# Row-maximum products of the next head, issued singly over the key steps

## The chip, the cores and the metric

The kernel runs on one core of a Trainium2 chip. The metric is the device time of one execution in microseconds; the median over several executions is compared. TensorE does the matmuls, VectorE (DVE) and GpSimd (POOL) elementwise work and reductions, ScalarE (ACT) the exponentials and copies, and SP issues most of the DMAs. Each engine works through its own list of instructions in order.

## The reference

Two layers over 2048 latent and 256 context tokens of width 1024. A layer normalises and modulates its input, projects it to 2816 columns, and runs four mixers: Fourier, attention, a short convolution and pooling. Each is gated by a SiLU; the gated outputs are concatenated and go through one output projection, and a residual is added. The part that matters here is the attention: four query heads of 64 channels on two key heads, for latent tokens

```python
sc = jnp.einsum('bqkgd,bskd->bkgqs', qi, k_all, preferred_element_type=jnp.float32)
p = jax.nn.softmax(sc, axis=-1).astype(v_all.dtype)
return jnp.einsum('bkgqs,bskd->bqkgd', p, v_all)
```

over all 2304 keys; context tokens attend to the 256 context keys alone, and only in the first layer.

## The kernel before

Tokens are in five blocks: block 0 has the 256 context tokens, blocks 1 to 4 have 512 latent tokens each. One head of one block is an object `Head` (called a head below): the first layer has 20 (blocks 1, 2, 3, 4, 0), the second 16. Numbers are split into a high and a low fp16 part, so a product takes two or three passes.

A head has two generators. `front` prepares it: one DMA loads its queries (qb), four transposes (L922) and a copy (L924) give qhh, then for each of four groups of 128 queries come five products with the keys (L931, one of 256 and four of 512 columns) and a reduction of each to row maxima (L932). Then comes the ending: the maxima are combined (L935), scaled into qb (L936), transposed (L939) and copied to qlm (L941). The maxima serve as the shift of the exponentials. `main` runs over the keys in 18 steps of 128 (2 steps for block 0). A step makes the scores in two matmuls (L972 with qhh, L973 with qlm, which brings the shift), two exponentials on ScalarE (L977, L978), a subtraction (L979, on GpSimd in even steps and on VectorE in odd ones) and the value products of the step before (L967) and of the one before that (L965). `back` and `close` normalise, gate and store a head's output while the next head runs.

PSUM has four tags with two banks each: st for scores, mx for the products of the maxima and for transposes, pv for value products, fl for what runs beside. `attention` runs the heads in turn and calls the next head's `front` from within `main`, at the steps of a tuple.

Beside the attention runs a fill: gates and local groups first (`local_groups`, L307), and later the output projection (`project`, L1125). It comes in groups of six matmuls of 512 columns. `spread` hands them out:

```python
past = [mark[0]] * (lag + 1)
for i in range(total):
    steps(gen, 1)
    past = past[1:] + [mark[0]]
    with tc.issue_after(past[0]), tc.issue_after(load_mark[0] or past[0]):
        steps(fill, n * (i + 1) // total - n * i // total)
```

`mark[0]` is the TensorE instruction that the source set last, a score's L972 or a product's L931, and `issue_after` keeps the fill's matmuls behind the mark of the step before (lag 1). The order on each engine is not that of the source: a scheduler takes instructions by their place in the source as soon as a model of the timeline finds them ready, within such edges.

The calls of a layer: `keys_values` loads keys in five steps and values in six; `opening` runs the first head's front under the value loads; then `spread(att, fill, ...)` runs all heads but those of the last two blocks beside the local groups. `project_setup` loads and splits w_out, 12 attention steps are run with no fill between, and then the remaining heads run beside the projection of the earlier blocks (96 groups over 71 steps in the first layer, 64 over 132 in the second). This place is called the takeover below.

Of the kernel before, what the change touches and what calls it, by code (L numbers as in the profile page):

```python
# [42 lines left out]
def hybrid_kernel(ctx: ExitStack, tc: tile.TileContext, T, out):  # L43
# [296 lines left out]
    def layer_blocks(L):  # L340
        return list(range(5)) if L == 0 else list(range(1, 5))
# [565 lines left out]
    class Head:  # L907
# [5 lines left out]
        def front(self):  # L913
            b, h, tp, kvs = self.b, self.h, self.tp, self.kvs
            g0, n = BLK[b]
            nt = n // 128
            kv = h // 2
            qb = tp.tile([128, 4, QW], F16, tag="qb", name="qb")[:, 0:nt]
            load_mark[0] = SP.dma_start(out=qb[:, :, 0:192], in_=qd[g0 // 128:(g0 + n) // 128, :, h].rearrange("t p c -> p t c")).ins
            pt = mx_bank(F16)  # L920
            for t in range(nt):
                PE.transpose(out=pt[:, t * 128:(t + 1) * 128], in_=qb[:, t, 0:128], identity=id16)  # L922
            qhh = tp.tile([128, 512], F16, tag="qhh", name="qhh")[:, 0:n]
            ACT.copy(out=qhh, in_=pt[:, 0:n])  # L924
            yield
            keys = [kvs["kc"][:, 0, kv, :]] + ([] if b == 0 else [kvs["kst"][kv][:, i * 512:(i + 1) * 512] for i in range(4)])
            mp = sm.tile([128, 4, 5], F32, tag="mp", name="mp")
            for t in range(nt):
                for i, kk in enumerate(keys):
                    ps = mx_bank()[:, 0:kk.shape[-1]]  # L930
                    mark[0] = PE.matmul(out=ps, lhsT=qhh[:, t * 128:(t + 1) * 128], rhs=kk, start=True, stop=True).ins  # L931
                    DVE.tensor_reduce(out=mp[:, t, i:i + 1], in_=ps, axis=AX.X, op=ALU.max)  # L932
                yield
            mr = sm.tile([128, 4], F32, tag="mr", name="mr")[:, 0:nt]
            DVE.tensor_reduce(out=mr, in_=mp[:, 0:nt, 0:len(keys)], axis=AX.X, op=ALU.max)  # L935
            DVE.tensor_scalar(out=qb[:, :, 192], in0=mr, scalar1=-1.0 / MROW, scalar2=PSHIFT * LOGIT / MROW, op0=ALU.mult, op1=ALU.add)  # L936
            pt = mx_bank(F16)
            for t in range(nt):
                PE.transpose(out=pt[0:65, t * 128:(t + 1) * 128], in_=qb[:, t, 128:193], identity=id16)  # L939
            qlm = tp.tile([128, 512], F16, tag="qlm", name="qlm")[:, 0:n]  # L940
            DVE.tensor_copy(out=qlm[0:65, :], in_=pt[0:65, 0:n])  # L941
            self.q = qhh, qlm
# [76 lines left out]
    def attention(heads):  # L1019

        o32 = [None]
        for _ in heads[0].front():
            yield
        for i, hd in enumerate(heads):
            ahead = heads[i + 1].front() if i + 1 < len(heads) else iter(())
            for j, _ in enumerate(hd.main()):
                if j == 1 and i:
                    heads[i - 1].back(o32)
                if j == (1 if heads[i].b == 0 else 3) and i:
                    heads[i - 1].close(o32)  # L1030
                if hd.b == 0 or j in (0, 2, 4, 7, 10, 13):
                    next(ahead, 0)
                yield
            yield from ahead
        heads[-1].back(o32)
        heads[-1].close(o32)

# [98 lines left out]
    def steps(gen, n):  # L1136
        for _ in range(n):
            if next(gen, 0) == 0:
                return

    def chain(*gens):
        for g in gens:
            yield from g
# [4 lines left out]
    with ExitStack() as st:  # L1148
        tp = TagPool(st, tc, "s0", {**TOKEN, "x": 4, "xn": 2, "h32": 2, "row": 1})
        ws = []  # L1150
        ahead = prep(0, 0, tp, aux_bank)
# [16 lines left out]
        for b in range(5):  # L1168
            ahead = prep(0, b + 1, tp, aux_bank) if b + 1 < 5 else iter(())
# [6 lines left out]
    def spread(gen, fill, total, n, lag=0):  # L1176
# [8 lines that stand above are left out]
    def weave(gen, n, other, m):  # L1185

        for i in range(n):
            steps(gen, 1)
            steps(other, m * (i + 1) // n - m * i // n)
            yield  # L1190
        yield from gen
        yield from other

    def opening(load, att):

        for i, _ in enumerate(load):
            if i < 5:
                steps(att, 1)
            yield 1

    for L in range(DEPTH):
        blocks = sorted(layer_blocks(L), key=lambda b: b == 0)
        nb = len(blocks)
        GATES = 148 * nb // 5
        zst = ExitStack()
        gates = gate_groups(L, TagPool(zst, tc, f"z{L}", {"z": 1}), gate_w[L])
        with ExitStack() as st:
            tags = {"acc0": 1, "acc1": 1, "part": 1} if L == 0 else {}
            tags.update({"u": 5, "wf": 1, "wm": 2, "t32": 3, "td": 3, "osb": 1, "dtab": 1, "tab": 1, "pq800": 1, "pq801": 1, "pq810": 1, "pq811": 1})
            if L:  # L1210
                tags.update({"dtab": 2, "tab": 2, "td": 4})
            fp = TagPool(st, tc, f"f{L}", tags)
            mods = chain(*(modulate(i, c, pv_bank, fp) for i, c in ([(0, 4), (0, 5)] + [(1, c) for c in range(6)] if L == 0 else [])))
            work = weave(fourier(L, fp), 24, mods, 32)
            steps(gates, 6)
            spread(work, gates, 24, GATES - 6, 4)
            steps(work, 1 << 30)
            if L == 0:
                affine(1)
        right = ExitStack()  # L1220
        ap = TagPool(right, tc, f"a{L}", {"zt": 2, "p32": 2, "qb": 2, "qhh": 2, "qlm": 2, "ph": 3, "pl": 3, "acc": 1, "o32": 1}, "right")
        kvs = {}
        att = attention([Head(L, kvs, b, h, ap) for b in blocks for h in range(4)])
        with ExitStack() as st:
            lp = TagPool(st, tc, f"l{L}", {"e": 8, "ht": 2, "hb": 2, "hu": 2, "pw32": 1, "pw": 2, "dh": 1, "dl": 1})
            fill = chain(gates, local_groups(L, lp))
            m = 8 * 4 * nb - GATES
            load = keys_values(L, ap, kvs)
            spread(load, fill, 5, 15, 0)
            spread(opening(load, att), fill, 6, 18, 1)  # L1230
            early = blocks[:-2]
            n, m = 72 * len(early), 8 * 4 * nb + 3 + m - 15 - 18
            spread(att, fill, 80, m * 80 // n, 1)
            with tc.issue_after(load_mark[0]):
                out_scale(L)
            spread(att, fill, n - 80, m - m * 80 // n, 1)
            steps(fill, 1 << 30)
        zst.close()
        with ExitStack() as st:
            tp = TagPool(st, tc, f"p{L}", {"mix": 1, "ml": 2, "ot": 1, "gate": 1, "x": 2})  # L1240
            project_setup(L, kvs)
            steps(att, 12)
            fill = project(L, early, tp)
            spread(att, fill, sum(72 if b else 11 for b in blocks[-2:]) - 12, sum(BLK[b][1] // 16 for b in early), 1)
            steps(fill, 1 << 30)
            steps(att, 1 << 30)
            right.close()
            late = project(L, blocks[-2:], tp)
            if L + 1 < DEPTH:
                with ExitStack() as st2:  # L1250
                    sp = TagPool(st2, tc, f"s{L + 1}", {**TOKEN, "s": 2, "x": 2, "xn": 1, "h32": 2}, "right")
                    with tc.issue_after(load_mark[0]):
                        block = token_groups(L + 1, sp, [])
                    for b in blocks[0:2]:
                        for _ in prep(L + 1, b, sp, mx_bank):
                            steps(late, 3)
                    for i, b in enumerate(blocks):
                        ahead = prep(L + 1, blocks[i + 2], sp, mx_bank) if i + 2 < 5 else iter(())
                        if i == 4:
                            gate_w[L + 1] = load_w(L + 1, *GATE_W[0:2], True)  # L1260
                        for _ in block(b):
                            steps(ahead, 1)
                            steps(late, 8)
                        steps(ahead, 9)
                        if i == 0:
                            steps(late, 1 << 30)
            steps(late, 1 << 30)
# [98 lines left out]
```

## Time and profile before

| what | us |
|---|---|
| median of 3 executions | 2276.16 |
| lowest and highest | 2273.22, 2279.15 |
| the profiled execution | 2273.57 |
| its span, first to last instruction | 2271.8 |
| TensorE, busy | 2158.7 |
| VectorE, busy | 1407.4 |
| ScalarE, busy | 1227.9 |
| GpSimd, busy | 936.1 |

The profile is of one execution. Busy time is the time in which an engine works on at least one instruction; a matmul of 512 columns shows some 380 ns, and the next one can start 0.22 us behind it, so the sum of durations says little. A wait is put down to the instruction that released the engine. The granted clock is the share of TensorE's full clock in a stretch.

### The profile page before, as it was taken

To read this page: it belongs to the slowest core of one execution; us is meant where nothing else is said; L and a number is where in the kernel's file an instruction comes from. 1 tells how busy PE (TensorE), PEld (TensorE's weight loads), DVE (VectorE), ACT (ScalarE), POOL (GpSimd) and SP (SyncE) were. 2 spreads that over 40 slices of the span, in tenths; PEclk is the share of its full clock that TensorE was granted. 3 is DMA by queue.
4 is the path that set the end of the run, shared out by engine and by line. 5 is a ranking of instruction groups with operands and counts; after the bars stand their busy time and mean duration, and the time that the engine had idled before them with its cause. 6 is when DMAs were issued, how large, how long until landed. Compare 5 with 4: busy or idle time off the path is not lost.

```text
span 2271.8 us, 41300 instructions
## 1 busy us (share of the span) xinstructions
PE 2158.7 (95%) x16327; PEld 1292.0 (57%) x16327; DVE 1407.4 (62%) x2639; ACT 1227.9 (54%) x2297; POOL 936.1 (41%) x996
## 2 busy tenths in 40 slices
PE   7999899989998999999999989999999999899999
PEld 3997556545555555545557984554454555455554
DVE  3655886366768767666465545413567776787743
ACT  4653454346777766544445624323467766566640
POOL 2786542215454455422125862011344556333320
PEclk9999999999999999999999999999999999999999
DMA  8424455510322110223474424323124210222133
GB/s 317 145 92 129 151 178 171 182 53 26 113 76 81 54 31 28 95 79 114 141 237 134 136 76 137 112 104 103 35 70 141 70 37 31 65 74 72 61 117 121
DMA packets 164081, 237.97 MB, mean 105 GB/s; under 512 B 28618, under 2 KB 113966, under 8 KB 163886
## 3 DMA queue, kind: packets, MB, share of 16 engines
q1 hardware_dynamic: 141294, 205.95, 27.2%
q10 hardware_dynamic: 22592, 29.37, 4.2%
q8 instruction: 128, 2.10, 0.4%
q14 instruction: 67, 0.55, 0.1%
HBM read 165.94 MB, written 69.34 MB: 104 GB/s over the span
## 4 chain that ended last, share of the span: by engine, by line
PE 68%; DVE 9%; ACT 4%; POOL 4%; issue 3%; DMA 2%; SPq 0%; POOLq 0%; DVEq 0%; ACTq 0%
PE fl L307 19%; PE fl L1125 15%; PE st L307 6%; PE pv L967 4%; PE st L972 4%; PE st L973 4%; PE mx L931 4%; DVE mp L932 2%; PE pv L965 2%; PE pv L329 1%; PE st L329 1%; PE mx L853 1%; DVE pl L979 1%; POOL pl L979 1%; PE mx L683 1%
## 5 line engine op out<-in xcount | busy, mean ns | idle before, releaser
L979 POOL TENSOR_TENSOR pl<-p,ph 128x512 f16<-128x512 f32 (+1 forms) x292 | 361.8, 1239 | 577.6 <-ACT p L978 515.1
L307 PE MATMUL fl<-h,w 128*128 128x512 f16 (+1 forms) x2592 | 582.1, 370 | 12.6 <-ACT w L147 9.3
L307 PEld LDWEIGHTS <-w 128*128 128x128 f16 x3456 | 331.5, 99 | 373.1 <-issue 22.2
L977 ACT ACTIVATE ph<-st 128x512 f16<-128x512 f32 (+1 forms) x584 | 350.9, 601 | 223.0 <-PE st L973 214.7
L932 DVE TENSOR_REDUCE mp<-mx 128x1 f32<-128x512 f32 (+1 forms) x648 | 388.8, 626 | 123.3 <-PE mx L931 112.7
L1125 PE MATMUL fl<-wo,ml 128*128 128x512 f16 x1632 | 376.8, 379 | 2.5 <-DVE ml L148 2.5
L978 ACT ACTIVATE p<-st 128x512 f32<-128x512 f32 (+1 forms) x584 | 351.2, 601 | 29.7 <-DVE pl L979 20.2
L979 DVE TENSOR_TENSOR pl<-p,ph 128x512 f16<-128x512 f32 (+1 forms) x292 | 231.9, 794 | 124.3 <-ACT p L978 100.0
L1125 PEld LDWEIGHTS <-ml 128*128 128x128 f16 x1632 | 157.4, 98 | 182.1 <-DVE ml L148 3.7
L967 PE MATMUL pv<-V,ph 128*128 128x130 f16 x2320 | 230.0, 221 | 6.9 <-ACT ph L977 6.2
L967 PEld LDWEIGHTS <-ph 128*128 128x128 f16 x2320 | 170.4, 98 | 116.4 <-ACT ph L977 29.1
L931 PE MATMUL mx<-kst,qhh 128*128 128x512 f16 x512 | 191.3, 385 | 22.9 <-DVE mp L932 22.1
L972 PE MATMUL st<-qhh,kst 128*128 128x512 f16 x512 | 195.6, 382 | 7.1 <-ACT p L978 6.2
L973 PE MATMUL st<-qlm,k 65*128 65x512 f16 x512 | 196.8, 384 | 0.0
L307 PE MATMUL st<-h,w 128*128 128x512 f16 (+1 forms) x864 | 189.1, 369 | 0.0
L965 PE MATMUL pv<-V,pl 128*128 128x66 f16 x2320 | 173.0, 194 | 12.5 <-DVE pl L979 6.0
L329 PEld LDWEIGHTS <-h 128*128 128x128 f16 x1632 | 160.0, 98 | 19.9 <-POOL h L269 1.1
L965 PEld LDWEIGHTS <-pl 128*128 128x128 f16 x2320 | 134.3, 98 | 65.0 <-POOL pl L979 14.0
L319 PEld LDWEIGHTS <-h 128*128 128x128 f16 x1728 | 99.5, 98 | 1.4 <-issue 0.6
L931 PEld LDWEIGHTS <-qhh 128*128 128x128 f16 x648 | 62.5, 99 | 65.8 <-issue 25.5
L329 PE MATMUL pv<-w,h 128*128 128x256 f16 x816 | 95.0, 275 | 0.9 <-POOL h L269 0.9
L329 PE MATMUL st<-w,h 128*128 128x256 f16 x816 | 92.7, 273 | 0.0
(303 smaller groups left out, 2903.7 us busy)
## 6 DMA issues: line engine op xcount, KB each, us to landing
wm<-in_w_mod_dram SPq DMA_DIRECT2D x48, 512.0 KB, 4.7
wst<-in_w_in_dram SPq DMA_DIRECT2D x44, 512.0 KB, 5.0
mix<-mixd SPq DMA_DIRECT2D x34, 512.0 KB, 4.0
zd<-z SPq DMA_DIRECT2D x64, 256.0 KB, 2.2
wst<-in_w_out_dram SPq DMA_DIRECT2D x32, 512.0 KB, 4.3
xt<-in_x_dram SPq DMA_DIRECT2D x20, 512.0 KB, 4.7
xd<-xt SPq DMA_DIRECT2D x18, 512.0 KB, 2.8
xt<-xd ACTq DMA_DIRECT2D x18, 512.0 KB, 3.7
```

What stands on the lines that cost most here:

```text
L307: PE.matmul(out=ps, lhsT=w[:, wp, k, :], rhs=h_ap(b, hp, k, 0, n), start=(k == 0 and i == 0), stop=(k == KC - 1 and i == 2))
L329: PE.matmul(out=ps[:, t], lhsT=h_ap(b, hp, k, (2 * i + t) * 128, 128), rhs=w[:, :, wp, k, :], start=(k == 0 and j == 0), stop=(k == KC - 1 ...
L931: mark[0] = PE.matmul(out=ps, lhsT=qhh[:, t * 128:(t + 1) * 128], rhs=kk, start=True, stop=True).ins
L932: DVE.tensor_reduce(out=mp[:, t, i:i + 1], in_=ps, axis=AX.X, op=ALU.max)
L965: PE.matmul(out=pv[t // 2][:, t % 2, 0:66], lhsT=p, rhs=v[:, 0:66], start=False, stop=(kt == nk - 1), skip_group_check=True)
L967: PE.matmul(out=pv[t // 2][:, t % 2, :], lhsT=p, rhs=v, start=(kt == 0 and t % 2 == 0), stop=False, skip_group_check=True)
L972: mark[0] = PE.matmul(out=ps, lhsT=self.k_tile(0, kt), rhs=qhh, start=True, stop=False).ins
L973: PE.matmul(out=ps, lhsT=self.k_tile(1, kt)[0:65, :], rhs=qlm[0:65, :], start=False, stop=True)
L977: ACT.activation(out=ph, in_=ps, func=ACTF.Exp, scale=1.0 / LOGIT)
L978: ACT.activation(out=p32, in_=ps, func=ACTF.Exp, scale=1.0 / LOGIT)
L979: (POOL if kt % 2 == 0 else DVE).tensor_tensor(out=pl, in0=p32, in1=ph, op=ALU.subtract)
L1125: PE.matmul(out=ps, lhsT=ml[:, mp, k, :], rhs=wo[k][:, wp, half * 512:(half + 1) * 512], start=(k == 0 and j == 0), stop=(k == KC - 1 and ...
```

## The change

`front` yields after each product and not after each group of five. `attention` takes 22 calls of the next front (4 if it is of block 0) and hands them out evenly over the key steps up to step 16 (up to step 1 in block 0). `opening` runs three calls of the first front under each of the six value loads, where it ran one under each of the first five. The number of steps of the first part of the attention grows by three, as three of the front's calls are left for it.

```diff
                     mark[0] = PE.matmul(out=ps, lhsT=qhh[:, t * 128:(t + 1) * 128], rhs=kk, start=True, stop=True).ins
                     DVE.tensor_reduce(out=mp[:, t, i:i + 1], in_=ps, axis=AX.X, op=ALU.max)
-                yield
+                    yield
...
-        for _ in heads[0].front():
-            yield
+        yield from heads[0].front()
         for i, hd in enumerate(heads):
             ahead = heads[i + 1].front() if i + 1 < len(heads) else iter(())
+            want = 2 + (2 if heads[i + 1].b == 0 else 20) if i + 1 < len(heads) else 0
+            last, done = 1 if hd.b == 0 else 17, 0
             for j, _ in enumerate(hd.main()):
...
-                if hd.b == 0 or j in (0, 2, 4, 7, 10, 13):
+                while done < want * (j + 1) // last:
                     next(ahead, 0)
+                    done += 1
                 yield
-            yield from ahead
+            for _ in ahead:
+                pass
...
-        for i, _ in enumerate(load):
-            if i < 5:
-                steps(att, 1)
+        for _ in load:
+            steps(att, 3)
             yield 1
...
-            n, m = 72 * len(early), 8 * 4 * nb + 3 + m - 15 - 18
+            n, m = 72 * len(early) + 3, 8 * 4 * nb + 3 + m - 15 - 18
```

## Rows read from the trace of the kernel before

**Rows 1.** The page's first part: busy us (share of the span) xinstructions.
```profile
PE 2158.7 (95%) x16327; PEld 1292.0 (57%) x16327; DVE 1407.4 (62%) x2639; ACT 1227.9 (54%) x2297; POOL 936.1 (41%) x996
```

**Rows 2.** Windows by stage: length, each engine's busy us, granted clock, DMA.
```profile
490.00:936.00 446.00, 426.46 (x3506) 245.00 (x3503) 316.17 (x518) 314.06 (x613) 228.73 (x244) 0.99 0.17 56
936.00:972.00 36.00, 30.32 (x186) 14.80 (x185) 26.06 (x47) 12.81 (x23) 6.11 (x6) 0.98 0.45 140
972.00:1160.00 188.00, 186.22 (x1265) 98.15 (x1264) 107.91 (x188) 86.71 (x163) 44.32 (x43) 0.98 0.38 125
1610.00:1940.00 330.00, 310.81 (x2477) 172.52 (x2474) 234.54 (x368) 230.09 (x445) 173.59 (x177) 1.00 0.20 67
1940.00:1968.00 28.00, 20.09 (x110) 8.61 (x109) 21.58 (x39) 8.88 (x17) 4.30 (x5) 0.87 0.33 106
1968.00:2190.00 222.00, 215.74 (x1815) 122.04 (x1815) 159.39 (x260) 144.70 (x277) 80.21 (x69) 0.99 0.19 62
```

**Rows 3.** Waits of TensorE, whole span: total us, times, longest us.
```profile
PE mx L931 <- DVE mp L932: 24.4, 57, 1.6
...
PE pv L965 <- DVE pl L979: 6.0, 9, 1.8
...
PE mx L939 <- DVE qb L936: 2.4, 2, 1.2
...
PE st L973 <- DVE qlm L941: 1.1, 4, 0.3
```

**Rows 4.** Waits of TensorE, first opening, 440 to 490 us.
```profile
PE mx L931 <- DVE mp L932: 2.9, 8, 1.2
```

**Rows 5.** Waits of TensorE, second opening, 1560 to 1610 us.
```profile
PE mx L931 <- DVE mp L932: 3.0, 10, 0.6
```

**Rows 6.** Waits of TensorE, first takeover, 936 to 972 us.
```profile
PE mx L931 <- DVE mp L932: 2.7, 5, 0.9
```

**Rows 7.** Waits of TensorE, second takeover, 1940 to 1968 us.
```profile
PE mx L931 <- DVE mp L932: 4.5, 8, 1.6
```

**Rows 8.** The page's costliest groups: busy, mean ns, idle before, releaser.
```profile
L932 DVE TENSOR_REDUCE mp<-mx 128x1 f32<-128x512 f32 (+1 forms) x648 | 388.8, 626 | 123.3 <-PE mx L931 112.7
```

**Rows 9.** Timeline, end of the first front: start us, us, engine, line.
```profile
485.48 0.38 PE L931 MATMUL mx<-kst,qhh 128*128 128x512 f16 x1 [0.30 <-DVE mp L932]
...
486.08 0.38 PE L931 MATMUL mx<-kst,qhh 128*128 128x512 f16 x1 [0.22 <-DVE mp L932]
...
487.85 0.17 DVE L935 TENSOR_REDUCE mr<-mp 128x4 f32<-128x20 f32 x1
488.06 0.18 DVE L936 TENSOR_SCALAR qb<-mr 128x4 f16<-128x4 f32 x1
...
489.48 0.39 PE L939 MATMUL mx<-id,qb 128*65 128x128 f16 x4
```

**Rows 10.** Timeline of TensorE, first takeover.
```profile
947.48 0.38 PE L931 MATMUL mx<-kst,qhh 128*128 128x512 f16 x1
949.06 4.27 PE L1125 MATMUL fl<-wo,ml 128*128 128x512 f16 x19 [1.20 <-DVE ml L148]
```

**Rows 11.** Windows around the two takeovers (PEclk is the granted clock).
```profile
964.00:980.00 16.00, 11.98 (x61) 5.59 (x59) 11.61 (x21) 5.80 (x11) 2.47 (x3) 0.79 0.29 76
1956.00:1974.00 18.00, 12.63 (x58) 5.40 (x58) 13.79 (x26) 4.82 (x9) 2.31 (x2) 0.72 0.15 41
```

**Rows 12.** Timeline of VectorE, first takeover.
```profile
954.20 1.28 DVE L148 SCALAR_TENSOR_TENSOR ml<-mix,f,ml 128x1024 f16<-128x1024 f32 x1 [3.53 <-ACT ml L147]
```

**Rows 13.** Timeline of VectorE at a handover from head to head.
```profile
815.93 0.41 DVE L941 COPY qlm<-mx 65x512 f16<-65x512 f16 x1
```

**Rows 14.** Timeline of TensorE at the same handover.
```profile
809.45 0.38 PE L931 MATMUL mx<-kst,qhh 128*128 128x512 f16 x1
...
813.54 0.38 PE L972 MATMUL st<-qhh,kc 128*128 128x512 f16 x1
813.76 1.46 PE L307 MATMUL fl<-h,w 128*128 128x512 f16 x6
```

## The prediction

> **What bounds the kernel now.** The page's first part comes first: TensorE is busy for 2158.7 us [rows 1] of the span of 2271.8, so all that a change of order can win lies in the remaining 113.1 us and in what the clock loses. Second, the windows by stage [rows 2] say how much of it lies in the attention after its openings. TensorE idles 19.5 us (446.0 less 426.46) while the first layer's heads run beside the gates and local groups, 5.7 where the projection takes over as their companion, 1.8 beside it, and 19.2, 7.9 and 6.3 in the same stages of the second layer: 60.4 us in all. VectorE is next at 316 of 446 us (71%), so it is not the bound over a stage, but it can be over a few steps. Third, the waits of TensorE [rows 3] name what ends these gaps. A product of the row maxima (L931) waits 24.4 us in all for the reduction of an earlier one (L932), since the tag mx has two banks. Of this 2.9 and 3.0 us lie in the two openings [rows 4, 5], 2.7 and 4.5 in the two takeovers [rows 6, 7], which leaves 11.3 for the running stages. The low-part value product (L965) waits 6.0 us for a subtraction on VectorE, which stands there behind reductions and other work.
>
> **What the change does.** It removes and adds no instruction: 648 reductions of 626 ns mean [rows 8] and as many products stay, and so do the transposes and the q load, one DMA per head on SP's queue, still at step 0. Four things move.
>
> One: within a head, 20 products were issued as four lumps of five, at steps 2, 4, 7 and 10, and the ending (L935 to L941) at 13. Now 22 calls go over 17 steps, one in twelve of them and two in five, and the ending comes at step 16, in the call right behind that of the last product. A lump costs this [rows 9]: the first two products find free banks, then each waits for a reduction, at 485.48, 486.08 and so on, 0.60 us apiece where TensorE issues matmuls of that size 0.22 us apart (19 in 4.27 us [rows 10]). It also holds the fill, because the mark of a step is its last product: the next step's fill matmuls may not be issued ahead of the fifth. One or two a step find both banks free unless VectorE is busy with something else. Of the 11.3 us I take two thirds off, 7.5, as the rest is VectorE at the fill's own work, and half of the subtractions' 6.0, 3.0. Bounds: nothing, since the scheduler places each instruction when its model finds it ready and may already have spread the lumps, and all 17.3. Taken: -10.5 us.
>
> Two: the first head's front. Five calls, four of them lumps, become 18 calls, three under each of six value loads, and three more in the first steps of the main loop. Of three products only the third finds no bank: six waits of 0.30 us [rows 9] make 1.8 against 2.9 and 3.0 now. Taken: -2.3 us for both layers; bounds 0 and -5.9. The three late products lie under two groups of six fill matmuls in those steps; without that cover they would cost 0.6 us each, 3.6 for both layers.
>
> Three: the takeover by the projection. The 12 steps that are run ahead of its fill held all 20 products of the next head; now they hold 14 (15 of 22 calls, the first without a product). The products are late there because their q load lies on SP's queue behind eight loads of w_out, and VectorE splits the projection's tiles as well. In the trace the fill runs out before the products do, and TensorE then issues products at VectorE's pace: 2.7 us of waits in the first layer, 4.5 in the second [rows 6, 7], and 1.2 in each ahead of L939 [rows 3]. The granted clock around them is 0.79 and 0.72 [rows 11], so (1 - 0.79) x 16 = 3.4 us and (1 - 0.72) x 18 = 5.0 us are lost to its lower level of 1.2 GHz. With six products moved behind the first fill, they run beside it. Against that, the fill may now start only behind the 14th product, whose mark stands where a score's stood. In the trace the seventh product is at 947.48 and the next on TensorE are 19 fill matmuls [rows 10]. At 0.60 us each, seven more take 4.2 us, of which the products are 1.5: 2.7 us of new idle time, or 6.2 if VectorE also stalls for the projection's next tile, as it did here for 3.53 [rows 12]. The first layer thus gains 7.3 less 2.7 to 6.2, so 1.1 to 4.6; the second 10.7 less as much, so 4.5 to 8.0. Since the new gap may itself lower the clock I take the lower parts, -2 and -4: -6 us. Bounds: -18.0, all of it, and +12.4, two gaps of 6.2 with nothing won.
>
> Four: the handover from head to head. The ending stood three steps behind the last product and five ahead of the next head's first score; now it is pressed into the last two. The chain is reduction, L935, L936, transposes, L941: 0.63 + 0.17 + 0.18 + 0.39 + 0.41 = 1.78 us of work [rows 8, 9, 13], more with queueing. Its cover is the fill of two or three steps, the last value products, and the new head's first half score (L972), which needs no maxima and whose mark sets the next fill free. The trace has such a case: a last product at 809.45, L941 at 815.93, and in between the new head's L972 at 813.54 with six fill matmuls behind it [rows 13, 14], and TensorE has no gap. Where a wait for L941 shows, it is 0.3 us [rows 3]. There are 30 handovers between full heads, 15 a layer. Between 0 and 1.78 us each I take 0.2, near the trace's own: +6 us; bounds 0 and 53. With the cover gone it is the 53.
>
> **Sum.** -10.5 - 2.3 - 6 + 6 = -12.8 us. The profiled execution took 2273.57 us, so 2260.8 by it; it stands 2.6 below the median of 2276.16, and the changed kernel's median is forecast at 2263.4, say 2263.
>
> **Rivals.** A: nothing that can be measured. For it: L931's waits are 57 in 648 products [rows 3, 8], so the scheduler already spreads most of them, and TensorE's work is unchanged. Then two and three are left, in part: 2270 to 2280. B: slower, by the handover. The next head's L973 waits for L941, TensorE has used up the fill of those steps, and the exponentials start late. It decides from 18.8 / 30 = 0.63 us per handover, 18.8 being what the other terms win; at half the chain, 0.89, it is 26.7 - 18.8 = +7.9, 2284, and at all of it +34.6, 2311. For it: the fill of the second layer's last heads is thin, 64 groups over 132 steps. Against: that handover without a gap [rows 14]. C: the takeover gets worse, since no fill passes the 14th product: +12.4 where I have -6, so +5.6 in all, 2282. Against: its present cost is already high [rows 11]. D: many short waits for banks in place of few long ones pull the clock down. In the two long running stages the granted clock is 0.99 and 1.00 [rows 2] although products wait there now; a fall as in the first takeover costs 3.4 us, so one at every fifth handover makes 20.4 and, less the 12.8, +7.6: 2284. The Trainium skill ("TensorE: Matmul & The Clock Gate", A second HAM failure mode: psum-queue depth-cycling) says that cycling through PSUM banks with short idle times between groups of matmuls makes the clock swing. By that page the change would be a loss; the trace so far bears it out around the takeovers, and hardly in the long stages.
>
> **How the numbers follow.** A change within 0.3%, some 7 us, is about what a measurement of this kernel can tell from none: 2269 to 2283. The forecast, faster than that, gets 0.52; A 0.24; B 0.14, C 0.06 and D 0.04, together 0.24. The likeliest case's own range is 2248 to 2269: half the far bounds of one and two (11.6) with all of three (18.0) and nothing lost at the handover is -29.6, 2247. Upward B at half the chain and D give 2284, and the range ends a little behind them, at 2286. About one in ten is left out on either side.
>
> **What would show it.** Right: the waits of L931 for L932 fall from 11.3 to about 4 us in the running stages and from 5.9 to about 4 in the openings; the takeover has its idle time around the 14th product and not before L939, and its granted clock rises; waits of L973 for L941 stay near 0.3 us each. Wrong: waits for L941, or of L939 for L936, at most handovers; a longer time per head; or waits of L931 that stay as they are, which would mean that the scheduler's order and not the source's had set them.

## The result and the profile after

The changed kernel takes 2250.76 us (median of 4 runs, 2249.6 to 2253.78) where the kernel before takes 2275.85 beside it (2273.22 to 2279.15). The ratio is 0.9896, with a 95% interval from 0.9877 to 0.9914: 25 us less, where 12.8 less was forecast. The direction was right and the time lies inside the range, but the gain is twice the forecast: term three came true for another reason than the one given, and 11 to 18 us come with an effect that no term had. That the forecast came this near is in part luck.

Line numbers up to 1022 are those of before; the projection's fill is now L1128 (before L1125) and the set-up's reduction L1048 (before L1045). First the page's part 1, to be read beside [rows 1]: busy us, share of the span, count.

```profile
PE 2154.2 (96%) x16327; PEld 1293.2 (58%) x16327; DVE 1412.8 (63%) x2639; ACT 1232.7 (55%) x2297; POOL 928.9 (41%) x996
```

The span fell from 2271.8 to 2248.7 us. TensorE's idle time went from 113.1 to 94.5 us, which is 18.6, and its busy time fell by 4.5 with the same 16327 matmuls: a matmul that stands alone counts for 0.38 us and one right behind another ends some 0.22 later, so fewer interruptions are part of that, and the clock may be another.

The second view is the waits of TensorE over the whole span of the changed kernel (total us, times, longest), to be read beside [rows 3]:

```profile
PE mx L931 <- DVE mp L932: 15.1, 30, 1.9
...
PE pv L965 <- DVE pl L979: 5.9, 10, 1.4
...
PE st L972 <- ACT p L978: 2.7, 6, 0.9
PE mx L939 <- DVE qb L936: 2.7, 4, 1.2
PE st L973 <- DVE qlm L941: 2.7, 10, 0.3
...
PE pv L967 <- ACT ph L977: 2.1, 5, 0.6
...
PE pv L965 <- POOL pl L979: 1.0, 3, 0.5
```

The same view of the kernel before, three rows that were not shown:

```profile
PE pv L967 <- ACT ph L977: 6.2, 13, 0.8
PE st L972 <- ACT p L978: 6.2, 9, 1.3
...
PE pv L965 <- POOL pl L979: 5.8, 8, 1.6
```

Products of the row maxima wait 15.1 us for reductions where they waited 24.4. The next four lines of the changed kernel are the same row in its two openings (440 to 493 and 1550 to 1604 us) and its two takeovers (925 to 960 and 1916 to 1941 us); they answer to [rows 4, 5, 6, 7]:

```profile
PE mx L931 <- DVE mp L932: 1.0, 2, 0.6
...
PE mx L931 <- DVE mp L932: 1.8, 3, 0.7
...
PE mx L931 <- DVE mp L932: 2.1, 5, 0.7
...
PE mx L931 <- DVE mp L932: 2.9, 7, 0.6
```

That leaves 7.3 us for the running stages, where 11.3 stood. The subtraction on VectorE that L965 waits for is unchanged (5.9 for 6.0). But the waits further down the softmax, which the prediction did not count, fell from 18.2 to 5.8 us: L972 and L967 for the exponentials on ScalarE, L965 for GpSimd's subtractions. Against that, products wait longer for the copy of the transposed queries (L931 for L924: 6.5 us, before 3.5).

To compare stages whose edges move, I cut both traces at the same pieces of work: a running stage reaches from the first score (L973) of a layer's first full head to that of the head in whose front the projection takes over, and the takeover from there to the first score of the head after it. Windows of the changed kernel (edges, length, PE, PEld, DVE, ACT, POOL busy, granted clock, DMA share, GB/s):

```profile
493.70:914.20 420.50, 404.65 (x3358) 233.73 (x3359) 311.20 (x502) 300.70 (x583) 215.84 (x230) 1.00 0.18 59
914.20:959.60 45.40, 38.95 (x288) 20.90 (x286) 29.92 (x58) 24.85 (x48) 16.02 (x15) 0.92 0.28 85
1604.00:1903.40 299.40, 291.43 (x2316) 162.68 (x2316) 221.89 (x349) 214.48 (x411) 156.70 (x162) 1.00 0.22 71
1903.40:1940.60 37.20, 30.91 (x230) 16.72 (x229) 29.04 (x53) 22.67 (x46) 17.08 (x16) 0.85 0.21 69
```

The same windows of the kernel before:

```profile
490.40:918.30 427.90, 411.46 (x3377) 235.47 (x3377) 303.68 (x504) 299.92 (x584) 215.13 (x232) 1.00 0.17 57
918.30:972.60 54.30, 45.71 (x315) 24.65 (x314) 38.65 (x62) 26.62 (x52) 19.70 (x18) 0.92 0.33 101
1611.20:1919.80 308.60, 294.06 (x2311) 162.59 (x2309) 219.62 (x349) 212.12 (x409) 157.23 (x163) 1.00 0.20 68
1919.80:1967.30 47.50, 34.98 (x266) 17.83 (x265) 35.64 (x57) 25.21 (x51) 20.13 (x18) 0.93 0.26 83
```

Length less PE busy is TensorE's idle time. All stages of the attention, cut in this way:

| stage | idle before, us | idle after, us | difference |
|---|---|---|---|
| openings, both layers | 7.7 + 6.1 | 6.5 + 5.1 | -2.2 |
| running stages | 16.4 + 14.5 | 15.8 + 8.0 | -7.1 |
| takeovers | 8.6 + 12.5 | 6.5 + 6.3 | -8.3 |
| beside the projection | 1.7 + 6.3 | 2.7 + 4.8 | -0.5 |

The differences add up to 18.1 of the 18.6 us. The lengths of the stages are not compared, because the stages hold different numbers of fill matmuls.

### The profile page after: what moved, and what is told of

Read it like the earlier page. It is cut to its first block, busy times and chain, and to the rows that moved or that the text cites. A ratio compares the mean times of both kernels' runs of the same rounds, so it can differ in the third digit from the quotient of the medians.

```text
span 2248.7 us, 41313 instructions
## 1 busy us (share of the span) xinstructions
PE 2154.2 (96%) x16327; PEld 1293.2 (58%) x16327; DVE 1412.8 (63%) x2639; ACT 1232.7 (55%) x2297; POOL 928.9 (41%) x996
## 5 line engine op out<-in xcount | busy, mean ns | idle before, releaser
L307 PE MATMUL fl<-h,w 128*128 128x512 f16 (+1 forms) x2592 | 595.3, 371 | 14.0 <-ACT w L147 10.4
L979 POOL TENSOR_TENSOR pl<-p,ph 128x512 f16<-128x512 f32 (+1 forms) x292 | 354.3, 1213 | 551.0 <-ACT p L978 480.9
L307 PEld LDWEIGHTS <-w 128*128 128x128 f16 x3456 | 331.9, 99 | 370.8 <-issue 21.6
L932 DVE TENSOR_REDUCE mp<-mx 128x1 f32<-128x512 f32 (+1 forms) x648 | 394.7, 628 | 160.3 <-PE mx L931 156.0
L1128 PE MATMUL fl<-wo,ml 128*128 128x512 f16 x1632 | 383.7, 382 | 2.9 <-ACT ml L147 2.9
L1128 PEld LDWEIGHTS <-ml 128*128 128x128 f16 x1632 | 159.1, 98 | 185.2 <-issue 6.4
L967 PEld LDWEIGHTS <-ph 128*128 128x128 f16 x2320 | 171.3, 98 | 111.3 <-ACT ph L977 14.1
L967 PE MATMUL pv<-V,ph 128*128 128x130 f16 x2320 | 227.2, 221 | 2.5 <-ACT ph L977 2.1
L931 PE MATMUL mx<-kst,qhh 128*128 128x512 f16 x512 | 190.4, 381 | 13.6 <-DVE mp L932 11.6
L972 PE MATMUL st<-qhh,kst 128*128 128x512 f16 x512 | 195.3, 381 | 3.6 <-ACT p L978 2.7
L973 PE MATMUL st<-qlm,k 65*128 65x512 f16 x512 | 196.8, 384 | 0.0
L307 PE MATMUL st<-h,w 128*128 128x512 f16 (+1 forms) x864 | 188.5, 368 | 0.0
L965 PE MATMUL pv<-V,pl 128*128 128x66 f16 x2320 | 167.1, 193 | 7.0 <-DVE pl L979 5.9
L965 PEld LDWEIGHTS <-pl 128*128 128x128 f16 x2320 | 131.8, 98 | 54.4 <-DVE pl L979 10.4
L1134 DVE TENSOR_TENSOR ot<-fl,gate 128x512 f32<-128x512 f32 x68 | 46.8, 689 | 83.3 <-PE fl L1128 83.3
L931 PEld LDWEIGHTS <-qhh 128*128 128x128 f16 x648 | 61.4, 98 | 59.9 <-ACT qhh L924 13.1
```

The source lines that it names most:

```text
L307: PE.matmul(out=ps, lhsT=w[:, wp, k, :], rhs=h_ap(b, hp, k, 0, n), start=(k == 0 and i == 0), stop=(k == KC - 1 and i == 2))
L965: PE.matmul(out=pv[t // 2][:, t % 2, 0:66], lhsT=p, rhs=v[:, 0:66], start=False, stop=(kt == nk - 1), skip_group_check=True)
L967: PE.matmul(out=pv[t // 2][:, t % 2, :], lhsT=p, rhs=v, start=(kt == 0 and t % 2 == 0), stop=False, skip_group_check=True)
L972: mark[0] = PE.matmul(out=ps, lhsT=self.k_tile(0, kt), rhs=qhh, start=True, stop=False).ins
L973: PE.matmul(out=ps, lhsT=self.k_tile(1, kt)[0:65, :], rhs=qlm[0:65, :], start=False, stop=True)
L979: (POOL if kt % 2 == 0 else DVE).tensor_tensor(out=pl, in0=p32, in1=ph, op=ALU.subtract)
```

## The experiments

Each kernel was timed in five rounds beside the kernel before; a ratio below is to that. The experiments ran in three groups, in which the kernel before took 2273.8 (e1 to e4), 2276.1 (e5 to e8) and 2275.8 us (e9 to e12), so small differences between groups are better read from the ratios. The expectations set letters to the theories. **S**: the gain comes from the products that stand singly in the steps of the main loop. **O**: it comes from the openings and the count of steps with them. **M**: what makes lumps dear is the mark, the last product of a lump, ahead of which no fill may be issued. **F**: the fill's place against the key steps matters. **U**: the takeover's length is set by the next head's query transposes, which stand on TensorE behind the projection's set-up. **L**: any new order of the source is another draw for the scheduler, worth some 10 us either way.

**e1: lumps again in the main loop, all else as in the changed kernel** (undoes terms one, three and four).

```diff
-                while done < want * (j + 1) // last:
+                goal = sum(k for s, k in ((0, 1), (2, 5), (4, 5), (7, 5), (10, 5), (13, 1)) if s <= j)
+                while done < (goal if want == 22 and (True) else want * (j + 1) // last):
```

> The changed kernel, but its main loop hands the next head's 22 calls out in lumps again, at steps 0, 2, 4, 7, 10 and 13; the opening stays as changed. Theory S (each place pays for itself: openings 3.7 us, running stages 11, takeovers 8.4, by the time that TensorE lost in each stage): nearly all of the gain goes, 2270 to 2274 us. Theory L (any new order of the source gives the scheduler another draw, worth some 10 us either way): anything from 2245 to 2275, and stages that lose time are not those where the lumps are. Theory O (the opening carries the gain, since everything behind it moves up): 2250 to 2256.

Measured 2277.51 us, ratio 1.0012 [1.0, 1.0025]. The whole gain is gone, so O falls as an explanation by itself. The time is 3.5 us above the range of S and 2.5 above that of L. Windows of this run, the two running stages and the first takeover:

```profile
494.40:916.90 422.50, 404.93 (x3353) 232.09 (x3354) 308.40 (x503) 298.81 (x582) 215.93 (x228) 1.00 0.18 58
916.90:971.70 54.80, 45.85 (x315) 24.65 (x314) 39.56 (x62) 26.63 (x52) 19.89 (x18) 0.92 0.33 100
1613.60:1925.80 312.20, 294.18 (x2298) 162.68 (x2297) 218.75 (x349) 212.61 (x410) 153.02 (x159) 0.99 0.20 67
```

The running stages idle 17.6 + 18.0 = 35.6 us, even more than before, and the takeover is as long as before, 54.8 us. The waits of the softmax (L972 and L967 for ScalarE, L965 for GpSimd) add up to 25.4 us in this run, where the kernel before has 18.2 and the changed one 5.8.

**e2: the opening of before, the main loop singly.**

```diff
-        for _ in load:
-            steps(att, 3)
+        for i, _ in enumerate(load):
+            if i < 5:
+                steps(att, 5 if i else 1)
...
-            n, m = 72 * len(early) + 3, 8 * 4 * nb + 3 + m - 15 - 18
+            n, m = 72 * len(early), 8 * 4 * nb + 3 + m - 15 - 18
```

> The changed kernel, but the first head's front is again one call and four lumps of five under the first five value loads. Theory S: 2254 to 2255 us, the openings losing 3 to 4 us in all and the other stages nothing. Theory O: 2265 to 2275. Theory L: 2240 to 2262, with differences outside the openings.

Measured 2267.05 us, 0.9959 [0.9944, 0.9974]: 16 us of the 25 are gone, though the openings themselves had saved only 2.2 us of idle time. That is O's range, not that of S or L, but e1 has shown that the opening is not enough by itself. The running stages idle 31.2 us here. Something that the opening sets reaches through the whole layer; e6, e7, e9 and e10 follow it up.

**e3: lumps only in the head whose front lies under the takeover.**

```diff
-                while done < want * (j + 1) // last:
+                goal = sum(k for s, k in ((0, 1), (2, 5), (4, 5), (7, 5), (10, 5), (13, 1)) if s <= j)
+                while done < (goal if want == 22 and (i == len(heads) - 8) else want * (j + 1) // last):
```

> The changed kernel, but the one head per layer under which the projection takes over hands out the next head's calls in lumps, so that all 20 products stand ahead of the projection's fill. Theory S (term three: the fill held behind the 14th product is what shortens the takeover): 2257 to 2260 us, the loss of 6 to 9 us within the two takeovers. Rival U (the takeover is shorter because the local groups end earlier against the heads, which lets the next head's queries be transposed earlier): 2250 to 2253, and those transposes stay at 12 to 14 us behind the head's first score.

Measured 2247.64 us, 0.9886 [0.9867, 0.9905]: no loss, where theory S had 2257 to 2260 us (the rival, U, had 2250 to 2253). In the source 20 products stand ahead of the projection's first matmuls here, and 14 in the changed kernel; the traces have it the other way round. TensorE's timeline of e3 at the first takeover, with the fifth product and the first matmuls of the projection, which come ahead of the sixth:

```profile
931.86 0.38 PE L931 MATMUL mx<-kst,qhh 128*128 128x512 f16 x1
...
933.89 1.04 PE L1129 MATMUL fl<-wo,ml 128*128 128x512 f16 x4 [0.60 <-ACT ml L147]
```

The changed kernel runs all 20 products first (its rows stand below, at term three). So it costs no time that shows whether five products or 20 come ahead of the fill, and term three's mechanism is wrong.

**e4: the ending back at step 13, except under the takeover.**

```diff
-            last, done = 1 if hd.b == 0 else 17, 0
+            last, done = 1 if hd.b == 0 else 17 if i == len(heads) - 8 else 14, 0
```

> The changed kernel, but the 22 calls go over 14 steps, so that the ending comes at step 13 as before, except under the takeover. Theory H (term four: the late ending costs up to 0.2 us at each of 30 handovers): 2244 to 2248 us, and the waits of L973 for L941 and of L939 for L936 fall to the level of before. Theory S without H: the denser products cost as much as the handover gains, 2249 to 2255 us, with more waits of L931 for L932.

Measured 2265.8 us, 0.996 [0.9946, 0.9974], 15 us slower than the changed kernel and in neither theory's range. The windows are the two takeovers and the stage beside the second projection:

```profile
912.10:963.30 51.20, 41.53 (x296) 22.17 (x295) 35.15 (x59) 25.99 (x51) 18.77 (x17) 0.90 0.26 80
1909.10:1951.00 41.90, 30.14 (x244) 15.80 (x243) 30.17 (x54) 25.01 (x50) 19.42 (x18) 0.93 0.24 73
1951.00:2179.60 228.60, 219.77 (x1824) 123.89 (x1823) 155.33 (x261) 145.69 (x276) 81.93 (x69) 0.98 0.20 63
```

The running stages idle 23.2 us, as in the changed kernel (23.8). The loss stands in the takeovers (9.7 + 11.8 us idle for 6.5 + 6.3) and in the last stage (8.8 for 4.8). The 0.6 us in the running stages are no measure of the ending alone: there the waits for it (L973 for L941, L939 for L936) fell from 3.0 to 0.5 us, but those of L931 for L932 rose from 6.9 to 12.7, since the products now lie more densely. The transposes of the takeovers (see e8) come 16.5 and 16.7 us behind the running head's first score, where the changed kernel has 11.8 and 13.9.

**e5: the lumps of e1 without their mark**, so that a step's fill is held by a score and not by the fifth product.

```diff
-                    mark[0] = PE.matmul(out=ps, ...).ins
+                    ins = PE.matmul(out=ps, ...).ins
+                    if self.marks:
+                        mark[0] = ins
```

Only the first head of a layer keeps its marks.

> The kernel of the first experiment (lumps in the main loop, opening as changed, 2277.5 us), but the products of all heads behind the first set no mark, so that the fill is no longer held behind the fifth product of a lump. Theory M (a lump costs because it holds the fill, which then ends late against the heads and makes the takeover late): 2253 to 2263 us, and the next head's queries at the takeover are transposed 12 to 14 us behind the head's first score instead of 19. Rival P (a lump costs by the waits for its banks and by the burst of reductions on VectorE, held fill or not): 2271 to 2280.

Measured 2275.66 us, 1.0003 [0.9994, 1.0013]: P's range, not M's. The running stages idle 28.6 us for e1's 35.6 and the transposes of the takeover (see e8) come 12.5 us behind the running head's first score for 19.3, but the stage beside the second projection pays it back; its window in e5:

```profile
1959.80:2191.60 231.80, 218.72 (x1801) 123.68 (x1801) 155.90 (x258) 145.50 (x276) 78.08 (x69) 0.96 0.19 59
```

and in e1:

```profile
1972.80:2193.10 220.30, 214.04 (x1802) 120.96 (x1802) 157.28 (x258) 143.94 (x276) 79.68 (x69) 0.99 0.19 62
```

13.1 us idle for 6.3, at a granted clock of 0.96 for 0.99. So the mark holds the fill and makes the transposes late, as M says (7.0 us of idle time in the running stages), but taking it away is no gain over all.

**e6 and e7: opening and place taken apart.** e6 has e2's opening, and three empty steps behind it, with 3 added to the count again:

```diff
         yield from heads[0].front()
+        for _ in range(3):
+            yield
```

> The kernel of the second experiment (first front in lumps under the loads, 2267 us), but with three empty steps ahead of the main loop, so that the fill has the same place against the key steps as in the changed kernel. Theory F (that kernel lost 12 of its 16 us because the fill moved by three key steps against the heads): 2252 to 2257 us. Rival Q (the lumps in the openings cost the 16 us themselves): 2264 to 2270.

e7 is the changed kernel with 21 calls under the value loads, so that none is left for the main loop, and without the 3:

```diff
-            steps(att, 3)
+            steps(att, 4 if i < 3 else 3)
...
-            n, m = 72 * len(early) + 3, 8 * 4 * nb + 3 + m - 15 - 18
+            n, m = 72 * len(early), 8 * 4 * nb + 3 + m - 15 - 18
```

> The changed kernel, but the whole first front (21 calls) is handed out under the six value loads, four under each of the first three and three under the rest, so that no call of it is left for the main loop and the fill stands three key steps earlier against the heads. Theory F: 2260 to 2268 us, with the losses in the running stages. Rival Q: 2249 to 2253.

Measured: e6 2256.09 us, 0.9914 [0.99, 0.9928], as F had it; e7 2268.5 us, 0.9968 [0.9959, 0.9978], half a us beyond F's range and far from Q's. With the products singly in the main loop the four cases make a square:

| | fill where it was | fill three key steps earlier against the heads |
|---|---|---|
| opening in lumps | 2267.05 (e2) | 2256.09 (e6) |
| opening singly | 2268.5 (e7) | 2250.76 (changed) |

On the direction: a step ahead of the first key step gives the fill a start, so three such steps put it earlier against the heads; the expectations of e7, e9 and e10 have earlier and later the wrong way round. In the running stages the changed kernel has 816 and 612 matmuls of the fill (L307) left, e7 828 and 624, so the start is two groups of six in each layer. By the counts that `spread` is given it shrinks to nothing towards the end of the local groups.

The place of the fill is worth 11.0 and 17.7 us; the opening's own form at most 5.3 and, in the old place, nothing. The running stages of e7:

```profile
495.20:923.90 428.70, 408.56 (x3369) 235.14 (x3369) 318.03 (x503) 300.69 (x585) 221.28 (x235) 1.00 0.18 58
1613.90:1922.60 308.70, 295.97 (x2320) 163.97 (x2320) 219.98 (x348) 214.56 (x410) 162.72 (x163) 0.99 0.21 68
```

They idle 20.1 + 12.7 = 32.8 us where the changed kernel's idle 23.8. Most of that is the old wait: L931 waits 8.2 + 6.3 us for reductions in these two stages, in the changed kernel 3.5 + 3.4. The row over the whole span of e7 (the changed kernel has 15.1, the kernel before 24.4):

```profile
PE mx L931 <- DVE mp L932: 22.9, 39, 2.2
```

So whether single products save this wait hangs on the place of the fill. The lumped main loop does not gain by the place: with the fill in the new place (e1) it takes 2277.51 us, in the old place (the kernel before beside it) 2273.81.

**e9 and e10: other places.** e9 has the three empty steps behind the changed kernel's own opening and 6 in the count; e10 runs 20 calls under the loads and counts 1.

```diff
-            n, m = 72 * len(early) + 3, 8 * 4 * nb + 3 + m - 15 - 18
+            n, m = 72 * len(early) + 6, 8 * 4 * nb + 3 + m - 15 - 18
```

> The changed kernel with three empty steps between the first head's front and the main loop, so that the fill stands six key steps later against the heads than with none of the front's calls left over (the changed kernel has three, the seventh experiment none). Theory F1 (the later the fill, the better): 2240 to 2250 us. Theory F2 (what counts is which work of the local groups meets which key step, with no direction in it): anywhere from 2250 to 2272, in the running stages. Theory F3 (the place is of no account and the seventh experiment lost elsewhere): 2249 to 2253.

```diff
-            steps(att, 3)
+            steps(att, 4 if i < 2 else 3)
...
-            n, m = 72 * len(early) + 3, 8 * 4 * nb + 3 + m - 15 - 18
+            n, m = 72 * len(early) + 1, 8 * 4 * nb + 3 + m - 15 - 18
```

> The changed kernel with 20 calls of the first front under the value loads (four, four, then three each), so that one is left for the main loop and the fill stands one key step later than with none. Theory F1: 2258 to 2266 us, between 2268.5 and 2250.8. Theory F2: from 2248 to 2272, not tied to the two neighbours. Theory F3: 2249 to 2253.

Measured 2255.99 us, 0.991 [0.9892, 0.9928], and 2259.41 us, 0.9925 [0.9911, 0.9939]. A shift of 0, 1, 3 and 6 steps takes 2268.5, 2259.4, 2250.8 and 2256.0 us: neither the more the better (F1), nor of no account (F3). F2, the form without a direction, is left, but its ranges hold almost any outcome, and so do L's: that these are two things was not shown. Which work of the fill meets which key step, and why three is best of the four, stays open.

**e8: half of the next head's front ahead of the projection's set-up.** This goes to the takeover's cause as e3 left it open.

```diff
+            steps(att, 6)
             project_setup(L, kvs)
-            steps(att, 12)
+            steps(att, 6)
```

> The changed kernel, but six of the 12 attention steps that are run at the takeover come ahead of the projection's set-up instead of behind it, so that the next head's queries need not wait for the set-up's reduction over all outputs of the local groups. Theory U (the takeover's length is set by when these queries are transposed): the transposes come 3 to 6 us behind the head's first score, and each takeover is 4 to 8 us shorter: 2236 to 2243 us. Rival V (the projection's tiles and the splits of w_out set its length): 2248 to 2254.

Why this was tried shows the timeline of the changed kernel at the takeover (start, us, engine, line), a row for each link of a chain:

```profile
925.15 0.22 ACT L337 ACTIVATION_READ_ACCUMULATOR W<-zp 128x1 f32 x1
...
925.49 0.22 DVE L1048 TENSOR_REDUCE q<-mxs 128x1 f32<-128x80 f32 x1
...
925.77 0.38 PE L120 MATMUL mx<-q,ones 128*128 128x1 f32 x2 [0.23 <-DVE q L1048]
...
926.01 0.38 PE L922 MATMUL mx<-id,qb 128*128 128x128 f16 x4
```

The last local group's output (L337) frees the set-up's reduction (L1048), that its two matmuls (L120), and only behind these in TensorE's order come the next head's query transposes (L922), from which its products follow. The same chain in the kernel before:

```profile
936.88 0.22 ACT L337 ACTIVATION_READ_ACCUMULATOR W<-zp 128x1 f32 x1
...
937.21 0.22 DVE L1045 TENSOR_REDUCE q<-mxs 128x1 f32<-128x80 f32 x1
...
937.49 0.38 PE L120 MATMUL mx<-q,ones 128*128 128x1 f32 x2 [0.23 <-DVE q L1045]
...
937.73 0.38 PE L922 MATMUL mx<-id,qb 128*128 128x128 f16 x4
```

Counted from the running head's first score, the transposes come 937.73 - 918.3 = 19.4 us late before and 926.01 - 914.2 = 11.8 after. In e8 (TensorE's timeline) they stand ahead of that score:

```profile
910.89 0.39 PE L922 MATMUL mx<-id,qb 128*128 128x128 f16 x4
...
911.56 0.38 PE L973 MATMUL st<-qlm,kc 65*128 65x512 f16 x1
```

e8 takes 2240.91 us, 0.9854 [0.9836, 0.9871], some 10 less than the changed kernel and within U's range. Its takeovers:

```profile
911.60:952.90 41.30, 36.88 (x287) 20.09 (x284) 30.67 (x59) 24.46 (x48) 16.55 (x15) 0.96 0.30 93
1896.40:1929.50 33.10, 26.12 (x226) 15.42 (x226) 27.47 (x53) 22.41 (x45) 17.35 (x16) 0.95 0.24 77
```

Each is 4.1 us shorter at nearly the same count of matmuls, and the granted clock is 0.96 and 0.95 for 0.92 and 0.85.

The prediction had another reason for late products, a q load (L919) behind the loads of w_out (L1057) on SP's queue. In the trace of the kernel before, SP's timeline has the last of these loads long ahead of that q load:

```profile
769.89 2.43 SPq L1057 DMA_DIRECT2D wst<-in_w_out_dram  x2
...
917.34 0.37 SPq L919 DMA_DIRECT2D qb<-qd  x1
```

The view of the tile qb from 917 to 938 us says when the load landed:

```profile
DMA to landing us min/median/max: 2.6/2.6/2.6
```

The queries were there some 18 us before their transposes at 937.73.

**e11: all of those twelve steps ahead of the set-up.**

```diff
+            steps(att, 12)
             project_setup(L, kvs)
-            steps(att, 12)
```

> The kernel of the eighth experiment (2240.9 us), but with all 12 attention steps ahead of the projection's set-up and none behind it. Theory U (what pays is that the queries and first products do not wait for the set-up): no further gain, 2238 to 2245 us. Rival W (the set-up itself then comes late, its weights are split behind 12 steps, and the fill starts late): 2246 to 2256.

Measured 2239.83 us, 0.984 [0.9824, 0.9855]. That is e8's time within the spread, and U's range: six steps had been enough. It has the lowest time of the study. Its stages do not compare with e8's: the second takeover is 41.9 us long for 33.1, but with 252 matmuls for 226.

**e12: e8's order in the kernel before**, with all its lumps.

> The kernel before the change, lumps and all, with six of its 12 attention steps ahead of the projection's set-up. Theory U: each takeover is 4 to 8 us shorter here too, 2260 to 2268 us. Rival X (lumps at the takeover hold all that is won, since the second half's ten products still wait in lumps of five): 2270 to 2278.

Measured 2258.0 us, 0.992 [0.9904, 0.9936]: 18 us won without the change, 2 more than U had at best. Its takeovers:

```profile
918.60:964.70 46.10, 41.81 (x313) 22.24 (x312) 35.72 (x61) 27.02 (x51) 20.68 (x18) 1.00 0.35 107
1910.60:1951.00 40.40, 31.59 (x266) 17.68 (x265) 32.85 (x58) 25.89 (x51) 20.65 (x18) 0.99 0.28 84
```

46.1 and 40.4 us long for 54.3 and 47.5 with as many matmuls (313 and 266 for 315 and 266), and the granted clock is near full. The first takeovers can be put in a row by how late the transposes come. With lumps and 313 to 315 matmuls: 19.3 us late, 54.8 us long (e1); 19.4, 54.3 (before); 12.5, 49.2 (e5); 0.8 ahead, 46.1 (e12). With single products and 287 to 296 matmuls: 16.5, 51.2 (e4); 11.8, 45.4 (changed); 0.7 ahead, 41.3 (e8). e5's row was not shown yet:

```profile
920.80:970.00 49.20, 43.24 (x314) 23.27 (x311) 35.98 (x63) 25.96 (x50) 17.12 (x16) 0.93 0.35 106
```

That the order of the front and the set-up sets this length is shown on both kernels; that it does so by the transposes' place behind L120 is read from the timelines, as e8 and e12 move six whole steps.

## Why the prediction was half right

**Term one, the running stages** (-10.5): the direction and the place were right, and e1 shows it: with lumps alone put back, nothing of the gain is left. The working was off in its parts. The waits of L931 there fell by 4.0 us (11.3 to 7.3) where 7.5 stood, those of L965 for VectorE's subtraction did not fall at all where 3.0 stood; instead 12.4 us went from the waits of L972, L967 and L965 for ScalarE and GpSimd over the whole span, which the prediction did not list. Over the running stages the idle time fell by 7.1 us. I had read the lump as a wait of the product; the trace after, and e1's with the lumps put back, show that a larger part had come out one engine further on. The holding of the fill by the mark, named but not costed, is 7.0 us of idle time by e5, though e5 as a whole is no faster than e1 beyond the spread.

**Term two, the openings** (-2.3): their idle time fell by 2.2, as worked out. The step that failed is the sentence on the three late products, which treated the 3 added to the count as nothing but three products under other cover. It moves the fill against the key steps, by two groups at the first score and less towards the end, and with single products that is worth 11.0 to 17.7 us (e2, e6, e7). Without it the single products win only some 7 to 9 us (e7, e2), less than the 12.8 forecast; with it 25. The two do not simply add: without single products the shift wins nothing (e1). So it was luck that the forecast of the whole was not further off. A change of a count in a spread was costed as the steps that it adds, and not as the shift of all that follow.

**Term three, the takeover** (-6): the gain was there, 8.3 us of idle time, for another reason. The changed kernel does run all 20 products ahead of the first fill, with 2.26 us of wait behind them, as TensorE's timeline has it:

```profile
944.47 0.38 PE L931 MATMUL mx<-kst,qhh 128*128 128x512 f16 x1 [0.22 <-DVE mp L932]
947.11 8.12 PE L1128 MATMUL fl<-wo,ml 128*128 128x512 f16 x30 [2.26 <-ACT ml L147]
955.06 0.39 PE L939 MATMUL mx<-id,qb 128*65 128x128 f16 x4
```

So no six products moved behind the fill, and by e3 their place makes no difference. What moved is that the local groups end earlier against the heads, so the set-up's reduction and with it the transposes come 7.6 us earlier (19.4 to 11.8) and 4.7 us in the second layer (18.6 to 13.9). The single products do that and not the shift: in e2 and e7, without it, the transposes of the first takeover come 12.0 and 11.9 us late. e8 and e12 show that the takeover's length hangs on this order. That the products were late because of the q load on SP's queue was argued from the order in the source, and the trace contradicts it (see e8); the chain through L1048 was not looked for. The sign named for this term, a higher granted clock at the takeover, did not come either: 0.92 as before in the first layer, 0.85 for 0.93 in the second.

**Term four, the handover** (+6): the waits named did appear, 1.6 us more of L973 for L941 (ten waits for four) and 1.5 us of L939 outside the takeovers, 3.1 in all, so 0.1 us per handover where 0.2 was taken. In e4 the waits of L973 are back at 1.4 us over the whole span, but its products lie more densely, so no run has the price of the late ending by itself.

**The rivals.** A (nothing) and B (slower by the handover) are refuted by the time and by the waits just named. C foresaw rightly that no fill passes the products, and wrongly that this would cost: the takeover got shorter. D is refuted in the long running stages: the granted clock there is 1.00 in both kernels. The rule of the Trainium skill ("TensorE: Matmul & The Clock Gate", A second HAM failure mode: psum-queue depth-cycling), by which the single products through two banks would have cost clock, is thus not borne out in these stages. At the takeovers D is not settled: the clock is 0.92 in both kernels in the first layer, and 0.85 where it was 0.93 in the second.

**What stays open** is why three key steps of shift are better than none, one or six, and why e4, with an earlier ending and denser products, has its transposes late at the takeover; the scheduler's order follows from all of it together, and no run here takes that apart. Nor is it shown that the place of the fill is more than another draw (L).

## What to carry to other kernels

Where work passes through two banks, issue it in single pieces between the steps, and read the price of a lump from the waits of every engine behind it, not from its own wait alone. When an edit changes the count over which another stream is spread, cost the shift of that whole stream, and try a few shifts: here three steps were worth 11 to 18 of the 25 us. Where two streams meet, look for the small instruction of the new stream that stands ahead of the old one's next step in an engine's order; moving twelve steps ahead of a set-up won 11 us here on top of the change and six of them 18 without it.

## What the runs showed of the hardware that had not been expected

The granted clock over a takeover rose where only the order of the set-up and the front was changed: from 0.92 and 0.85 in the changed kernel to 0.96 and 0.95 in e8, and from 0.92 and 0.93 in the kernel before to 1.00 and 0.99 in e12, with practically the same matmuls (below 1.00 a part of the stretch ran at 1.2 GHz instead of 2.4). Earlier transposes alone are no rule for it: from the kernel before to the changed one they come 4.7 us earlier in the second layer, and the clock fell there from 0.93 to 0.85. And TensorE's busy time is no constant of the work: 16327 matmuls took 2168.8 us in e5, 2154.2 in the changed kernel and 2144.7 in e11, as the first part of the page says for e5:

```profile
PE 2168.8 (95%) x16327; PEld 1296.0 (57%) x16327; DVE 1399.2 (61%) x2639; ACT 1231.8 (54%) x2297; POOL 923.8 (41%) x996
```

and for e11:

```profile
PE 2144.7 (96%) x16327; PEld 1290.2 (58%) x16327; DVE 1412.8 (63%) x2639; ACT 1233.2 (55%) x2297; POOL 927.5 (41%) x996
```

So a forecast that goes by idle time alone misses a part: of the 23.1 us by which the span fell here, 4.5 were busy time.
